# Second pass of the 64-dim head logits: 128 rows in place of 64, with hi and lo of the keys in both halves of the rows

## The chip, the cores and the metric

The kernel runs on one core of one Trainium2 chip. The metric is the time of one execution in microseconds (us), as the device measures it; the time of a kernel is the median of its runs. A profile is one execution taken by the hardware profiler. Its span is the time from the first to the last instruction of the program, and the time of a run is somewhat longer than the span.

## The reference

One layer of a streaming encoder on 512 tokens of width 1024, in float32. The same normalised input feeds three token mixers: sparse attention (branch A, 8 heads of 64), stick-breaking attention (branch B, 8 heads of 64) and cross-attention into 256 memory tokens (branch C, 4 heads of 128). Sigmoid gates merge them, and a gated feed-forward layer follows. Cut to the three places where logits of 64-dim heads are computed:

```python
def dsa_attention(aq, ak, av, iq, ik, iw, rel_bias):              # branch A
    s = einsum('bqhd,bkd->bqhk', iq_b, ik) * IDX_DIM ** -0.5      # 8 index heads of 64, one shared key
    score = einsum('bqh,bqhk->bqk', iw_b, relu(s))
    score = where(admissible[None], score, -inf)
    _, idx = top_k(score, k_sel)                                  # 128 keys of a query
    logits = einsum('bqhd,bqkhd->bhqk', aq_b, kg) * HEAD_DIM ** -0.5
    logits = logits + bias                                        # by distance, per head
    p = softmax(where(valid, logits, -inf))
    return einsum('bhqk,bqkhd->bqhd', p, vg)

def stick_breaking_attention(bq, bk, bv):                         # branch B
    z = einsum('bqhd,bkhd->bhqk', q_b, bk) * HEAD_DIM ** -0.5
    causal = kpos[None, :] < qpos[:, None]
    log_beta = log_sigmoid(z)
    log_one_minus = where(causal, log_sigmoid(-z), 0.0)
    tail = reversed_cumsum(log_one_minus) - log_one_minus
    a = where(causal, exp(log_beta + tail), 0.0)
    return einsum('bhqk,bkhd->bqhd', a, bv)

x = x + rmsnorm((g_a * ya + g_b * yb + g_c * yc) @ w_out, g_mix_post)
gu = rmsnorm(x, g_ffn_pre) @ w_ffn_in
x = x + rmsnorm((silu(gu[..., :D_FF]) * gu[..., D_FF:]) @ w_ffn_out, g_ffn_post)
```

## The kernel before

**Exact products.** Every float32 operand is split into two float32r parts, hi and lo (`split`, lines 73 to 75: a copy on ScalarE, ACT, gives hi, and a subtraction on VectorE, DVE, gives lo). A product takes three matmuls on TensorE (PE): hi with hi, hi with lo, lo with hi (`passes`, lines 81 to 87). The lines L85, L86 and L87 in the profile are these three; L206 to L208 and L731 are the same for products with tokens on the output rows. Weights come by DMA from the queue of SyncE (SP) into three buffers `wraw` (line 95) and are split into two buffers each of `wh` and `wl`.

**Logits of 64-dim heads.** Here the contraction has only 64 rows. A head's queries are therefore kept with hi in one half of the 128 rows and lo in the other (`evac_q`): the even head of a pair has hi in the lower rows, the odd head in the upper ones. One matmul of 128 rows against the hi part of the keys, which stands in both halves, gives q_hi k_hi + q_lo k_hi (line 175). A second matmul adds q_hi k_lo, on the 64 rows that hold q_hi (line 176):

```python
self.nc.tensor.matmul(out, lhsT=x[:, s], rhs=k[h % 2][:, 0:n], start=True, stop=False)
self.nc.tensor.matmul(out, lhsT=x[r, s], rhs=lo[r, 0:n], start=False, stop=True)
```

The keys come from `evac_k` for branches A and B: four tiles of two heads each. The even head's hi part goes to the lower half of one half of an `act` slot (a tile of 128 x 1024, 22 buffers), the odd head's to the upper half of the other half, and a DMA from SP copies each to the opposite half of the rows (lines 168 and 169, 64 x 512 numbers, 128 KB each). The lo parts lie in a tile `klo` of 128 x 512 (5 buffers). In the indexer the one key is shared by all heads: `index_keys` keeps hi and lo side by side in one `act` slot and copies both to the other half with one DMA (line 459), but the second pass still reads 64 rows.

**Where these pairs of matmuls stand.** There are 88. The indexer (`scores`, lines 463 to 487) has 24: 8 heads by 3 query tiles, with n = 256, 384 and 512 keys. Branches A and B have 32 each: 8 heads by 4 query tiles, with n = 128, 256, 384 and 512 keys (`heads`, lines 558 to 576).

**Order of the work.** The order on PE is that of the code (`manual_schedule`). DVE, ACT, POOL (GpSimdE) and the DMA queue of SP are put in order by a scheduler from its own costs. Independent products stand in a queue of generators, and `fill(us)` issues some of them on PE after each logits step to cover the wait for the softmax of that step. The probabilities of a head are transposed by PE (line 531), split into tiles `pt` by ACT and DVE, and multiplied with the values (line 546) one head later.

**The selection.** After the scores of a query tile, `select` finds its 128 best keys by 16 rounds of maximum and replacement on DVE (lines 502 and 503). DVE also makes all lo parts, those of the weights that PE works on meanwhile among them.

Of the kernel before, what the change touches and what calls it, by code (L numbers as in the profile page):

```python
# [17 lines left out]
P = 128  # L18
T = 512
# [16 lines left out]
# First distance of each of the 16 buckets of the relative bias.  # L36
# [3 lines left out]
def rel_onehot():  # L40
    """[32, 640] one-hot of the bucket of rel = 127 - column (a constant of the shapes)."""
    rel = 127 - np.arange(REL)
    b = np.searchsorted(np.asarray(BUCKET_START), np.abs(rel), side="right") - 1
    b = b + np.where(rel > 0, 16, 0)
    return (np.arange(32)[:, None] == b[None, :]).astype(np.float32)


class Layer:
# [32 lines left out]
    def passes(self, out, pairs, first, last):  # L81
        """out (+)= sum over pairs of (stationary hi, lo, moving hi, lo)."""
# [7 lines left out]
    def load(self, src, kc, c, tag=None):  # L90
        """src: [kc*128, c] in DRAM -> float32 tile [128, kc, c]."""
# [6 lines left out]
    def parts(self, raw, tags=None, eng=None):  # L98
        """(hi, lo) tiles of a loaded tile."""
# [10 lines left out]
    def fill(self, us):  # L110
        """issue queued work of about us microseconds."""
# [9 lines left out]
    def drain(self, *gens):  # L121
        """issue all queued work up to the last of gens (all of it without gens)."""
        while self.queue and (not gens or any(g in self.queue for g in gens)):
            self.fill(1.0)

    def mix(self, a, b, n=1):
        """b, with n steps of a after each of its steps."""
# [13 lines left out]
    def feat(self, out, w, acts, kc=NK, n=T, **kw):  # L141
        """out[c, n] = w^T acts, contraction over kc*128 features."""
# [9 lines left out]
    # Logits of 64-dim heads: hi and lo of the queries of a head fill the 128 rows of the stationary  # L152
    # operand, against the hi part of the keys in both halves; a second pass on 64 rows has the lo part
    # of the keys. The even head keeps its hi part in the lower rows, the odd one in the upper rows.
# [7 lines left out]
    def evac_k(self, ps):  # L162
        slot = self.big("act")
        e, o = slot[:, 0:T], slot[:, T:2 * T]
        lo = self.att.tile([P, T], F32R, name="klo", tag="klo", bufs=5)
        self.split(e[0:64], lo[0:64], ps[0:64])
        self.split(o[64:128], lo[64:128], ps[64:128])
        self.nc.sync.dma_start(e[64:128].bitcast(F32), e[0:64].bitcast(F32))
        self.nc.sync.dma_start(o[0:64].bitcast(F32), o[64:128].bitcast(F32))
        return e, o, lo  # L170

    def head_logits(self, out, q, k, s, h, n):
        x, lo = q[h % 2], k[2]
        r = slice(64 * (h % 2), 64 * (h % 2) + 64)
        self.nc.tensor.matmul(out, lhsT=x[:, s], rhs=k[h % 2][:, 0:n], start=True, stop=False)  # L175
        self.nc.tensor.matmul(out, lhsT=x[r, s], rhs=lo[r, 0:n], start=False, stop=True)  # L176

    def feat_tiles(self, w_src, acts, out, js, n=T, t0=0, evac=None):
        """feature-major (hi, lo) of 128-column blocks js of w_src into out[j]."""
# [14 lines left out]
    def tok_tiles(self, w_src, acts, toks, out, heads=0):  # L194
        """token-major product with [1024, 512] weights for the token tiles toks; with heads, out[t]
        is one tile of (hi, lo) per head, side by side."""
# [23 lines left out]
    def squares(self, halves, both=False):  # L220
        """[128, 2] parts of the mean square of a row, of two halves of it; on both engines if wanted."""
# [9 lines left out]
    def rstd(self, ss):  # L231
        """-2 (mean + EPS) ** -0.5 of the two parts of the mean, with one Newton step."""
# [17 lines left out]
    def normed(self, x):  # L250
        """x * rstd(x) (gain not applied)."""
# [6 lines left out]
    def run(self):  # L258
# [4 lines left out]
        with self.tc.manual_schedule(engines={mybir.EngineType.PE}):  # L263
# [6 lines left out]
            # the first 128 queries have at most 128 admissible keys: all of them are selected  # L270
# [33 lines left out]
    def setup(self):  # L304
# [11 lines left out]
        # stick-breaking: ones where key == query, sliced per query tile  # L316
# [13 lines left out]
        # relative bias by distance, times 8  # L330
# [20 lines left out]
    def transposed(self, xs, k, g, hi, lo):  # L351
        """(hi, lo) of the transposes of columns 128k.. of the token tiles xs, times the gain g."""
# [6 lines left out]
    def first(self, x, row, w_ik, w_cq):  # L359
        """h^T by halves of the tokens, with the products of the first two weight blocks after each."""  # L360
# [88 lines left out]
    def index_keys(self, cq):  # L449
        nc = self.nc  # L450
        # shared key and head weights; first block of the queries of branch C
# [3 lines left out]
        self.ik = kh, kh, kl  # L455
# [33 lines left out]
    def select(self):  # L489
        """additive masks: 0 for the 128 best admissible keys of a query, -BIG elsewhere."""  # L490
# [33 lines left out]
    def values_T(self, p, b, pT):  # L524
        """transposes of the key blocks that share bank b; p[i]: [128 queries, 128(i+1) keys]."""
# [11 lines left out]
    def values(self, pT, v, h, out):  # L537
        """out^T rows of head h = V^T P^T: V hi and lo side by side as one stationary operand."""
# [19 lines left out]
    def heads(self, prob, v, out, gap, first):  # L558
        """prob(h, i): probabilities of a query tile. The products with the values of a head come one
        head later, and queued work fills the waits."""  # L560
# [310 lines left out]
```

## Time and profile before

Three runs took 961.47, 961.82 and 962.75 us. The span of the profiled execution is 960.9 us; its own run time isn't given beside the span, and the three runs lie 0.6 to 1.9 us above that span, the median 0.9 us.

| what | value |
|---|---|
| median of the runs | 961.82 us |
| span of the profiled execution | 960.9 us |
| PE, matmuls | busy 938.7 us (98%), 4426 instructions |
| PEld, weight loads of PE | busy 760.5 us (79%), 4426 instructions |
| DVE | busy 534.3 us (56%) |
| ACT | busy 404.6 us (42%) |
| POOL | busy 107.0 us (11%) |
| DMA | 98.95 MB, 103 GB/s on the mean |
| mean granted clock of PE | 0.997 |

Consecutive matmuls overlap in the records: a matmul's recorded duration holds the time until its last result is out, while the next one has already begun. What a matmul costs in a row of them is the distance from its start to the start of the next, called its pitch here. A record such as `64*128 64x512` names the stationary operand first (64 rows by 128 columns) and then the moving one (64 rows by 512 columns). A stationary operand is loaded by an instruction of its own (PEld, LDWEIGHTS).

The stages around the change, by time from the start of the span: the indexer's pairs run from 50 to 86 us, the selection on DVE goes on until 200 us while PE works on branch C and on the projections of branch A, PE does queued products until 244 us, branch A's pairs stand between 244 and 353 us and those of branch B between 353 and 462 us.

### The profile page before, as it was taken

How to read it: one execution, taken by the hardware profiler on the slowest of the kernel's cores; microseconds unless marked ns; L12 is line 12 of the kernel's file. 1: busy time of each engine (PE TensorE's matmuls, PEld its weight loads, DVE VectorE, ACT ScalarE, POOL GpSimd, SP SyncE). 2: the span in 40 equal slices, each digit the busy share in tenths (PEclk: the TensorE clock that was granted, in tenths of full speed). 3: DMA queues.
4: the chain of work that ended last, by engine and by line, in shares of the span. 5: the costliest groups of instructions: out<-in, count | busy, mean ns of one | idle time of the engine just before them, and what ended most of it. 6: DMA issues, size and time to landing. Idle time of an engine off the chain costs nothing.

```text
span 960.9 us, 11731 instructions
## 1 busy us (share of the span) xinstructions
PE 938.7 (98%) x4426; PEld 760.5 (79%) x4426; DVE 534.3 (56%) x920; ACT 404.6 (42%) x705; POOL 107.0 (11%) x147
## 2 busy tenths in 40 slices
PE   5999999999999999999999999999999999999997
PEld 4967888888777777777788888988888888888885
DVE  7568999963587876667544477333333333322225
ACT  5354575432666555655443355322223223212122
POOL 4000000010022303334222102000000000000000
PEclk9999999999999999999999999999999999999999
DMA  7423542343343322122283536023333233332202
GB/s 226 124 63 103 154 138 78 99 110 110 109 134 109 99 67 77 44 56 66 73 267 99 176 106 201 1 76 101 88 101 97 88 102 97 110 106 92 66 23 87
DMA packets 129532, 98.95 MB, mean 103 GB/s; under 512 B 4652, under 2 KB 115292, under 8 KB 129476
## 3 DMA queue, kind: packets, MB, share of 16 engines
q1 hardware_dynamic: 128884, 97.16, 33.9%
q10 hardware_dynamic: 592, 1.05, 0.3%
q8 instruction: 34, 0.56, 0.2%
q14 instruction: 22, 0.18, 0.1%
HBM read 93.73 MB, written 2.12 MB: 100 GB/s over the span
## 4 chain that ended last, share of the span: by engine, by line
PE 88%; DVE 6%; issue 2%; DMA 1%; ACT 1%; POOL 1%; SPq 0%; DVEq 0%; POOLq 0%; ACTq 0%
PE bank L85 20%; PE bank L87 20%; PE bank L86 20%; PE bank L731 14%; PE bank L176 3%; DVE wl L75 3%; PE bank L531 2%; PE bank L546 2%; PE bank L175 2%; PE bank L206 1%; PE bank L208 1%; PE bank L207 1%; DMA act<-in_x_dram 1%; DVE score L503 1%; DMA lraw<-in_w_ffn_in_dram 1%
## 5 line engine op out<-in xcount | busy, mean ns | idle before, releaser
L75 DVE TENSOR_TENSOR wl<-wraw,wh 128x1024 fp32r<-128x1024 f32 (+1 forms) x131 | 155.1, 1185 | 177.6 <-ACT wh L74 173.2
L74 ACT CAST wh<-wraw 128x1024 fp32r<-128x1024 f32 (+1 forms) x131 | 127.2, 972 | 229.4 <-PE bank L86 163.1
L85 PE MATMUL bank<-h,wh 128*128 128x512 f32 (+1 forms) x528 | 209.6, 397 | 0.0
L87 PE MATMUL bank<-h,wl 128*128 128x512 f32 (+1 forms) x528 | 204.7, 388 | 1.0 <-DVE wl L75 0.9
L86 PE MATMUL bank<-h,wh 128*128 128x512 f32 (+1 forms) x528 | 204.4, 387 | 0.0
L87 PEld LDWEIGHTS bank<-h,wl 128*128 128x128 f32 x528 | 99.1, 188 | 22.0 <-DVE wl L75 1.7
L85 PEld LDWEIGHTS bank<-h,wh 128*128 128x128 f32 x528 | 99.3, 188 | 20.0 <-issue 1.2
L86 PEld LDWEIGHTS bank<-h,wh 128*128 128x128 f32 x528 | 99.4, 188 | 17.8
L74 ACT CAST lwh<-lraw 128x1024 fp32r<-128x1024 f32 x36 | 37.9, 1052 | 119.4 <-PE bank L86 76.2
L731 PE MATMUL bank<-lwh,act 128*128 128x512 f32 x240 | 72.6, 393 | 0.0
L731 PE MATMUL bank<-wh,act 128*128 128x512 f32 x240 | 72.5, 393 | 0.0
L75 DVE TENSOR_TENSOR lwl<-lraw,lwh 128x1024 fp32r<-128x1024 f32 x36 | 44.1, 1224 | 43.1 <-ACT lwh L74 41.3
L85 PE MATMUL bank<-h,lwh 128*128 128x512 f32 x152 | 60.1, 396 | 0.0
L86 PE MATMUL bank<-h,lwh 128*128 128x512 f32 x152 | 60.1, 396 | 0.0
L87 PE MATMUL bank<-h,lwl 128*128 128x512 f32 x152 | 60.1, 395 | 0.0
L238 POOL TENSOR_TENSOR rs<-ms,mhalf 128x1 f32<-128x1 f32 x18 | 10.4, 579 | 423.9 <-DVE ms L237 419.9
L820 DVE TENSOR_TENSOR silu<-silu,bank 128x512 f32<-128x512 f32 x22 | 15.1, 686 | 76.4 <-PE bank L87 73.6
L595 POOL TENSOR_TENSOR p<-toep,score 128x128 f32<-128x128 f32 (+3 forms) x32 | 29.8, 944 | 218.4 <-DVE score L504 112.3
L731 PEld LDWEIGHTS bank<-wh,act 128*128 128x128 f32 x240 | 45.1, 188 | 10.0
L731 PEld LDWEIGHTS bank<-lwh,act 128*128 128x128 f32 x240 | 45.1, 188 | 9.9
L74 ACT CAST act<-bank 64x512 fp32r<-64x512 f32 (+3 forms) x63 | 34.8, 552 | 38.1 <-DVE act L75 16.7
L85 PE MATMUL bank<-act,wh 128*128 128x512 f32 (+1 forms) x128 | 48.6, 380 | 0.0
(161 smaller groups left out, 1616.6 us busy)
## 6 DMA issues: line engine op xcount, KB each, us to landing
wraw<-in_w_in_dram SPq DMA_DIRECT2D x64, 512.0 KB, 3.5
wraw<-in_w_ffn_in_dram SPq DMA_DIRECT2D x22, 512.0 KB, 3.7
lraw<-in_w_ffn_in_dram SPq DMA_DIRECT2D x22, 512.0 KB, 3.7
wraw<-in_w_ffn_out_dram SPq DMA_DIRECT2D x11, 512.0 KB, 3.7
lraw<-in_w_ffn_out_dram SPq DMA_DIRECT2D x11, 512.0 KB, 3.4
wraw<-in_w_mem_kv_dram SPq DMA_DIRECT2D x8, 512.0 KB, 3.4
lraw<-in_w_out_dram SPq DMA_DIRECT2D x6, 512.0 KB, 6.3
wraw<-in_w_out_dram SPq DMA_DIRECT2D x6, 512.0 KB, 4.0
```

Of the source, the lines that this page charges most:

```text
L74: self.nc.scalar.copy(hi, src)
L75: (eng or self.nc.vector).tensor_tensor(lo, src, hi.bitcast(F32), op=OP.subtract)
L85: self.nc.tensor.matmul(out, lhsT=sh, rhs=mh, start=first and i == 0, stop=False)
L86: self.nc.tensor.matmul(out, lhsT=sh, rhs=ml, start=False, stop=False)
L87: self.nc.tensor.matmul(out, lhsT=sl, rhs=mh, start=False, stop=last and i == n - 1)
L175: self.nc.tensor.matmul(out, lhsT=x[:, s], rhs=k[h % 2][:, 0:n], start=True, stop=False)
L176: self.nc.tensor.matmul(out, lhsT=x[r, s], rhs=lo[r, 0:n], start=False, stop=True)
L531: self.nc.tensor.transpose(ps[:, c:c + P], p[i][:, j * P:(j + 1) * P], self.ident)
L546: nc.tensor.matmul(ps[:, j * P:T], lhsT=w, rhs=part[:, o:o + n], start=j == 0 and i == 0, stop=j == NT - 1 and i == 1)
L595: nc.gpsimd.tensor_tensor(s, toep[0][:, 0:n][:, ::-1], self.mask[i], op=OP.add)
L731: self.nc.tensor.matmul(ps[c], lhsT=st_[:, s], rhs=mv_[:, 0, c * 512:(c + 1) * 512], start=f and k == order[0], stop=l and k == order[-1])
L820: nc.vector.tensor_tensor(sg, sg, pss[1], op=OP.mult)
```

## The change

- `evac_k` keeps hi and lo of the keys of a head side by side in one tile of 128 x 1024: the even head in an `act` slot as before, the odd head in a tile `ko` (5 buffers) that takes the place of `klo`. Each is copied whole to the opposite half of the rows, by a DMA of 64 x 1024 numbers (256 KB). The copy of a head now waits for its lo part as well, which DVE writes.
- `head_logits` uses all 128 rows in the second matmul too, with the same stationary operand as the first. It adds q_hi k_lo + q_lo k_lo; the last term was left out before.
- In the indexer nothing more is copied: hi and lo of the key already stood in both halves.
- `ko` is twice as large as `klo`. The kernel is built with `dynamic_dma_scratch_size=1024`, where the setting was left at its default before.
- Comments and docstrings are gone, and line numbers move by up to 3.

```diff
     def evac_k(self, ps):
-        slot = self.big("act")
-        e, o = slot[:, 0:T], slot[:, T:2 * T]
-        lo = self.att.tile([P, T], F32R, name="klo", tag="klo", bufs=5)
-        self.split(e[0:64], lo[0:64], ps[0:64])
-        self.split(o[64:128], lo[64:128], ps[64:128])
-        self.nc.sync.dma_start(e[64:128].bitcast(F32), e[0:64].bitcast(F32))
-        self.nc.sync.dma_start(o[0:64].bitcast(F32), o[64:128].bitcast(F32))
-        return e, o, lo
+        e, o = self.big("act"), self.att.tile([P, 2 * T], F32R, name="ko", tag="ko", bufs=5)
+        for x, a, b in ((e, slice(0, 64), slice(64, 128)), (o, slice(64, 128), slice(0, 64))):
+            self.split(x[a, 0:T], x[a, T:2 * T], ps[a])
+            self.nc.sync.dma_start(x[b].bitcast(F32), x[a].bitcast(F32))
+        return e, o
 
     def head_logits(self, out, q, k, s, h, n):
-        x, lo = q[h % 2], k[2]
-        r = slice(64 * (h % 2), 64 * (h % 2) + 64)
-        self.nc.tensor.matmul(out, lhsT=x[:, s], rhs=k[h % 2][:, 0:n], start=True, stop=False)
-        self.nc.tensor.matmul(out, lhsT=x[r, s], rhs=lo[r, 0:n], start=False, stop=True)
+        x, y = q[h % 2][:, s], k[h % 2]
+        self.nc.tensor.matmul(out, lhsT=x, rhs=y[:, 0:n], start=True, stop=False)
+        self.nc.tensor.matmul(out, lhsT=x, rhs=y[:, T:T + n], start=False, stop=True)
...
     def index_keys(self, cq):
-        self.ik = kh, kh, kl
+        self.ik = ik, ik
...
 def kernel(**inputs):
-    nc = bacc.Bacc("TRN2", target_bir_lowering=False, num_devices=1)
+    nc = bacc.Bacc("TRN2", target_bir_lowering=False, num_devices=1, dynamic_dma_scratch_size=1024)
```

The scheduler leaves nearly all of the order as it was. Two places show what moves.

The first is the DMA queue of SP around the first two key tiles of branch A (the first lies in `act_1572`, with the change in `act_1572` and `ko_1573`; the second in `act_1673`; `wraw` are weight loads). Before:

```order
L95 DMA wraw_1681<-in_w_in_dram 128x8x128 [waits DMAHW1_49,DVE_49]
L95 DMA wraw_1717<-in_w_in_dram 128x8x128 [waits DMAHW2_49,DVE_49]
L168 DMA act_1572<-act_1572 64x512 [waits Activation_49]
L95 DMA wraw_1756<-in_w_in_dram 128x8x128 [waits DMAHW3_49,DVE_49]
L169 DMA act_1572<-act_1572 64x512 [waits Activation_49]
L95 DMA wraw_1792<-in_w_in_dram 128x8x128 [waits DMAHW4_49,DVE_49]
L168 DMA act_1673<-act_1673 64x512 [waits Activation_49]
L169 DMA act_1673<-act_1673 64x512 [waits Activation_49]
```

And with the change:

```order
L95 DMA wraw_1681<-in_w_in_dram 128x8x128 [waits DMAHW1_49,DVE_49]
L95 DMA wraw_1717<-in_w_in_dram 128x8x128 [waits DMAHW2_49,DVE_49]
L95 DMA wraw_1756<-in_w_in_dram 128x8x128 [waits DMAHW3_49,DVE_49]
L167 DMA act_1572<-act_1572 64x1024 [waits DVE_49]
L167 DMA ko_1573<-ko_1573 64x1024 [waits DVE_49]
L95 DMA wraw_1792<-in_w_in_dram 128x8x128 [waits DMAHW4_49,DVE_49]
L167 DMA act_1673<-act_1673 64x1024 [waits DVE_49]
L95 DMA wraw_1831<-in_w_in_dram 128x8x128 [waits DMAHW5_49,DVE_49]
```

The copies wait for DVE instead of ACT, and one weight load (`wraw_1756`) moves ahead of the first copy.

The second is PE at the second head of branch A, for the first query tile (n = 128; `p` are the first head's probabilities, which the four matmuls of L531, L528 with the change, transpose). Before:

```order
L87 MATMUL bank<-act,wl 128x512
L175 MATMUL bank<-act 128x128
L176 MATMUL bank<-klo,act 128x128
L531 MATMUL bank<-ident,p_2339 128x128
L531 MATMUL bank<-ident,p_2371 128x128
```

And with the change:

```order
L87 MATMUL bank<-act,wl 128x512
L172 MATMUL bank<-ko,act 128x128
L173 MATMUL bank<-ko,act 128x128
L528 MATMUL bank<-ident,p_2339 128x128
L528 MATMUL bank<-ident,p_2371 128x128
```

On PE nothing moves: 4426 matmuls in the same order, with another operand in these places.

## The prediction

> **What bounds the kernel now.** I read the page's busy times and its chain of waits first, then busy times by stage, then the timeline of PE around the pairs, because only there can one see what a single matmul costs in a row of others.
>
> ```profile
> span 960.9 us, 11731 instructions
> PE 938.7 (98%) x4426; PEld 760.5 (79%) x4426; DVE 534.3 (56%) x920; ACT 404.6 (42%) x705; POOL 107.0 (11%) x147
> PE 88%; DVE 6%; issue 2%; DMA 1%; ACT 1%; POOL 1%; SPq 0%; DVEq 0%; POOLq 0%; ACTq 0%
> ```
>
> PE is busy nearly always and makes 88% of the chain that ended last, so time taken out of PE's row of matmuls comes out of the end, as far as the engines that feed it keep up. By stage (each row: the stretch, its length, then busy us and instructions of each engine):
>
> ```profile
> core 0: us, PE busy (x) PEld busy (x) DVE busy (x) ACT busy (x) POOL busy (x), PEclk, DMA share, GB/s
> 50.00:86.00 36.00, 36.00 (x164) 24.70 (x164) 25.23 (x52) 19.41 (x40) 0.00 (x0) 1.00 0.20 59
> 86.00:200.00 114.00, 113.74 (x557) 95.13 (x556) 110.86 (x251) 62.19 (x114) 2.05 (x5) 1.00 0.40 116
> 200.00:244.00 44.00, 43.93 (x194) 36.08 (x193) 15.94 (x18) 12.93 (x17) 4.63 (x5) 1.00 0.38 108
> 244.00:353.00 109.00, 109.00 (x502) 82.62 (x502) 85.43 (x196) 67.37 (x133) 22.99 (x24) 1.00 0.38 108
> 353.00:462.00 109.00, 109.00 (x509) 82.92 (x507) 73.54 (x93) 62.81 (x127) 36.37 (x65) 1.00 0.22 62
> 279.80:294.40 14.60, 14.60 (x70) 11.17 (x69) 12.16 (x28) 10.36 (x21) 4.54 (x5) 1.00 0.61 163
> ```
>
> In branch A (244 to 353) and branch B (353 to 462) PE has no idle time and DVE has 23.6 and 35.5 us to spare. From 86 to 200 us, in the selection, DVE is nearly full too (110.9 of 114.0): there two engines bind at once, which matters for the indexer's pairs just before.
>
> **What a pair costs.** The first tile of branch A with 512 keys, on PE and on its weight loads:
>
> ```profile
> 252.57 0.39 PE L87 MATMUL bank<-act,wl 128*128 128x512 f32 x1
> 252.79 0.39 PE L175 MATMUL bank<-act 128*128 128x512 f32 x1
> 253.11 0.49 PE L176 MATMUL bank<-klo,act 64*128 64x512 f32 x1
> 253.53 0.50 PE L85 MATMUL bank<-act,wh 128*128 128x512 f32 x1
> 253.87 0.39 PE L86 MATMUL bank<-act,wh 128*128 128x512 f32 x1
> 254.10 0.40 PE L87 MATMUL bank<-act,wl 128*128 128x512 f32 x1
> ...
> 252.57 0.19 PEld L175 LDWEIGHTS bank<-act 128*128 128x128 f32 x1
> 253.11 0.18 PEld L176 LDWEIGHTS bank<-klo,act 64*128 64x128 f32 x1 [0.35 <-issue]
> 253.53 0.19 PEld L85 LDWEIGHTS bank<-act,wh 128*128 128x128 f32 x1 [0.24 <-issue]
> ```
>
> L87 to L175 and L86 to L87 show the plain pitch of a matmul of 128 rows and 512 columns: 0.22 to 0.23 us; I use 0.228. From L175 to L176 it is 0.32, from L176 to L85 0.42 and from L85 to L86 0.34. The three take 1.08 us where three plain ones take 0.684: 0.396 us too much. The loads say why. The load of L175 begins 0.22 us before its matmul, under the matmul ahead of it; those of L176 and of the L85 behind it begin together with their matmuls. So the array finishes what it holds at each change between 128 and 64 rows, and the next load is not hidden. Two passes of 128 rows, like L85 and L86, which also share a stationary operand and a bank, show none of this.
>
> The indexer shows the same sum in a full period (L175, L176 and six matmuls of 256 columns):
>
> ```profile
> 78.60 0.28 PE L86 MATMUL bank<-act,wh 128*128 128x256 f32 x1
> ...
> 79.19 0.39 PE L175 MATMUL bank<-act 128*128 128x512 f32 x1
> 79.52 0.49 PE L176 MATMUL bank<-act 64*128 64x512 f32 x1
> 79.94 0.39 PE L85 MATMUL bank<-act,wh 128*128 128x256 f32 x1
> ...
> 80.75 0.40 PE L175 MATMUL bank<-act 128*128 128x512 f32 x1
> ```
>
> From 78.60 to 79.19 five matmuls of 256 columns take 0.59, so 0.118 each. The period takes 1.56 us, and plainly it would take 2 x 0.228 + 6 x 0.118 = 1.164: 0.396 too much again. The recorded durations don't tell this (0.49 against 0.39); starts do.
>
> Narrow pairs have less to give, since what follows is slow in itself:
>
> ```profile
> 256.39 0.22 PE L175 MATMUL bank<-act 128*128 128x128 f32 x1
> 256.54 0.32 PE L176 MATMUL bank<-klo,act 64*128 64x128 f32 x1
> 256.79 0.66 PE L531 MATMUL bank<-ident,p 128*128 128x128 f32 x4
> 257.20 0.48 PE L85 MATMUL bank<-act,wh 128*128 128x512 f32 x1
> ...
> 146.13 0.60 PE L655 MATMUL bank<-ident,p 128*128 128x128 f32 x4
> 146.49 0.49 PE L85 MATMUL bank<-h,wh 128*128 128x512 f32 x1
> ```
>
> A pair of 128 columns and four transposes take 0.81 us. Four transposes with no 64-row matmul ahead take 0.36 (146.13 to 146.49). A plain pitch at 128 columns I estimate at 0.11, close to the 0.118 at 256 columns, below which the load of 128 columns seems to bind. So 0.81 - 0.36 - 0.22 = 0.23 comes free. It also shows that ahead of transposes the third step brings 0.05 (0.41 against 0.36) where it brings 0.11 ahead of L85 (0.34 against 0.228).
>
> How many there are:
>
> ```profile
> L176 PE MATMUL bank<-klo,act x64: 323/409/501, 244.2 to 461.9; 64*128 64x128 f32 x16, 64*128 64x256 f32 x16, 64*128 64x384 f32 x16, 64*128 64x512 f32 x16
> L176 PE MATMUL bank<-act x24: 379/440/500, 50.8 to 84.9; 64*128 64x256 f32 x8, 64*128 64x384 f32 x8, 64*128 64x512 f32 x8
> ```
>
> **Sum on PE.** Indexer: 24 x 0.396 = 9.5 us. Branches A and B: 48 wide pairs x 0.396 = 19.0, less 28 of them followed by transposes (7 heads x 2 branches x n = 256 and 384) x 0.06 = 1.7, plus 16 narrow pairs x 0.23 = 3.7: 21.0 us. PE gets 30.5 us shorter. Bounds of the new second pass: at best it has the plain pitch, as every other pass of 128 rows; at worst its load is exposed as that of L176 is now, 0.18 us by the row above, which takes 15.8 us from the gain (a rival below). I take the best, since it becomes the same kind of pair as L85 and L86.
>
> **What hides, what comes late.** In the indexer the logits go from PE by ACT to DVE. PE would need 36.0 - 9.5 = 26.5 us there, and DVE has 25.2 us of work in it, with waits for ACT that don't vanish. Then comes the selection, where DVE has only 3.1 us to spare and PE already waits for it here and there:
>
> ```profile
> PEld bank L207 <- DVE wl L75: 1.0, 3, 0.5
> PEld bank L546 <- DVE pt L75: 0.6, 1, 0.6
> ```
>
> So what DVE doesn't gain by 86 us, PE gives back in the selection, waiting for lo parts of weights. DVE can start earlier by at most its idle time, 10.8 us from 50 to 86. With 1 to 3 us of it staying as latency, the indexer keeps 9.5 us at best and some 4 at worst (DVE as late as now in half of the stretch); I take 8.3.
>
> In A and B the fullest head (279.8 to 294.4) has DVE at 12.16 of 14.6 us; its four pairs give 0.23 + 2 x 0.336 + 0.396 = 1.3, which leaves 13.3 us, 91% of them DVE's. The wait of L546 for `pt` shows that DVE is at times just in time. I charge 0.8 us for such waits, 0 to 4 as the range. So 20.2 us stay, and 28.5 in all: the span becomes 932.4, and with the 0.9 us by which the median of the runs shown (961.82) lies above the span, **933.3 us**.
>
> **The copies.** The prices that the trace has (SP's DMAs, the count, KB each, median us to landing; DVE's lo part of a key; and what SP's loads wait for):
>
> ```profile
> act<-act SPq DMA_DIRECT2D x16, 128.0 KB, 2.2
> act<-act SPq DMA_DIRECT2D x1, 256.0 KB, 3.0
> wraw<-in_w_in_dram SPq DMA_DIRECT2D x64, 512.0 KB, 3.5
> lraw<-in_w_out_dram SPq DMA_DIRECT2D x6, 512.0 KB, 6.3
> L75 DVE TENSOR_TENSOR klo<-bank,act x16: 676/688/695, 156.8 to 364.3; 64x512 fp32r<-64x512 f32 x16
> SPq L95 <- DVE wl L75: 389.5, 87, 34.9
> ```
>
> ACT, DVE and PE get no instruction more, and the DMAs stay 16. Each carries 256 KB, like the indexer's copy now: 0.8 us later. Each is also issued after DVE's lo part, 0.69 us or a few DVE instructions later, and the weight loads behind it on SP with it. Those loads wait 389.5 us in total for buffers that DVE frees, so they are issued as early as buffers allow; with three buffers and 24 matmuls (5.5 us) per block, an estimate of the lead is 3 x 5.5 - 3.5 for landing - 2 for the split = 11 us. A delay of 1 to 3 us lies within it: nothing. Without that cover it would cost up to 16 x 1.5 = 24 us. The copies themselves are needed when branch A starts at 244 us, 40 us after the last of A, and for B one head or more after they land: nothing.
>
> **The Trainium skill.** The page "TensorE: Matmul & The Clock Gate" speaks against this change: its section "Why this matters for your kernels" says that a single matmul with a small contraction takes as long as one with 128 rows, and "LDWEIGHTS (loading the stationary operand)" that a load of 32 rows takes as long as one of 128. The trace agrees on the load (0.18 against 0.19 us), and by that rule the time stays near 962. But "TensorEngine Tiling (Array Packing)", section "Key Properties", says that changing the tiling mode drains the array, and the starts above side with it.
>
> **Rivals.**
> *The selection takes the indexer's gain* (DVE binds from the first scores on, and PE waits in the selection for the lo parts of weights). For it: DVE at 110.9 of 114. Against: DVE idles 10.8 us before it, waiting for what PE makes. Only A and B gain: 961.8 - 20.2 = 941.6.
> *The second pass still exposes its load.* Against: L86 at plain pitch. 933.3 + 15.8 = 949.1. In the skill, "The mechanism" on the first page has a load overlap running matmuls only when row groups differ, which would make it so; the load of L175 under L87 contradicts it.
> *Rows are not the cause*, and something else at these places (the first write of a bank, the operand's place) makes the steps. Against: L85 starts a bank as well, elsewhere without steps. Then 961.8.
> *Slower: the smaller DMA scratch throttles the loads.* If they could no longer be prepared ahead, a load that lands later than the 5.5 us in which PE uses a block makes PE wait at every block. At the 6.3 us of `lraw` and with the 64 loads of `w_in` alone: 64 x 0.8 = 51 us, so 933 + 51 = 984. It decides from 5.5 + 28.5/64 = 5.95 us to landing. For it: the change makes that scratch smaller. Against: nothing in the trace shows that a load uses it.
>
> **How the numbers follow.** The forecast has a chance of 0.74, with a range of its own from 929 (no loss at all: 961.8 - 30.5 = 931.3, and 2 us for narrow pairs and waits that I priced too low) to 938 (the indexer keeps 4, and A and B lose 1.5). The selection's rival has 0.14, the exposed load 0.04, no effect 0.04, slower 0.04. For 8 in 10 the range reaches into the selection's rival: 928.5 to 942. A measurement of this kernel tells 0.2% (1.9 us) from no change. Faster: 0.74 + 0.14 + 0.04 = 0.92; same 0.04; slower 0.04.
>
> **What would show it.** L172 to L173 and on to the next matmul at 0.23 us for 512 columns, with the load of L173 starting before its matmul; the stretch of branch A at about 99 us instead of 109, that of B the same; the indexer's at 26 to 30; DVE idle time between 50 and 86 us mostly gone; the rest of the span unchanged. I am wrong if L173 keeps a pitch over 0.3, if waits for `wl` or `pt` grow by more than 3 us, or if loads of `wraw` land later than 5 us.

## The result, and the profile after

Four runs of the changed kernel took 932.92 to 935.14 us, with a median of 933.41. Four runs of the kernel before on the same chip took 961.47 to 962.75 us, with a median of 962.23. The ratio is 0.9711, with a 95% interval from 0.9697 to 0.9724: 2.9% faster. The profiled execution has a span of 933.3 us against 960.9.

From the page of the changed kernel (span, busy times, and the shares of the chain that ended last):

```profile
span 933.3 us, 11731 instructions
PE 908.5 (97%) x4426; PEld 761.9 (82%) x4426; DVE 531.7 (57%) x920; ACT 402.5 (43%) x705; POOL 109.0 (12%) x147
PE 85%; DVE 8%; issue 2%; ACT 2%; DMA 1%; POOL 1%; POOLq 0%; DVEq 0%; SPq 0%; ACTq 0%
```

The number of instructions is the same and every engine but PE has about the same work as before. PE's busy time fell by 30.2 us, from 938.7; the span fell by 27.6. DVE's share of the chain rose from 6% to 8%.

Busy times by stage of the changed kernel, in the stretches that were shown of before:

```profile
core 0: us, PE busy (x) PEld busy (x) DVE busy (x) ACT busy (x) POOL busy (x), PEclk, DMA share, GB/s
50.00:86.00 36.00, 36.00 (x226) 32.30 (x225) 32.09 (x67) 23.54 (x47) 0.00 (x0) 1.00 0.33 100
86.00:200.00 114.00, 113.66 (x535) 93.88 (x534) 108.24 (x240) 60.82 (x110) 4.88 (x9) 1.00 0.44 123
244.00:353.00 109.00, 108.21 (x552) 91.61 (x552) 91.16 (x198) 73.95 (x146) 27.49 (x30) 1.00 0.44 119
353.00:462.00 109.00, 106.42 (x538) 89.20 (x537) 73.76 (x93) 59.70 (x121) 39.84 (x63) 1.00 0.29 85
```

The stretches are the same in time and not in work: in the changed kernel the last pair of the indexer starts at 77.4 us, the pairs of branch A begin at 236.4 us and those of branch B stand between 343.7 and 435.2 us. The first 36 us now hold 226 matmuls instead of 164, and the 109 us from 244 us on 552 instead of 502. In the last stretch PE is no longer busy all the time: 2.6 us of 109 are idle, where nothing was idle before.

A pair with 512 keys and one with 128 keys on PE, in branch B of the changed kernel (start, duration, line, shapes):

```profile
422.49 0.39 PE L87 MATMUL bank<-h,wl 128*128 128x512 f32 x1
422.72 0.39 PE L172 MATMUL bank<-act 128*128 128x512 f32 x1
422.95 0.40 PE L173 MATMUL bank<-act 128*128 128x512 f32 x1
423.18 1.09 PE L543 MATMUL bank<-pt,act 128*128 128x512 f32 x5
...
427.78 0.22 PE L172 MATMUL bank<-ko,act 128*128 128x128 f32 x1
427.84 0.28 PE L173 MATMUL bank<-ko,act 128*128 128x128 f32 x1
427.95 0.62 PE L528 MATMUL bank<-ident,p 128*128 128x128 f32 x4
428.33 0.48 PE L85 MATMUL bank<-h,wh 128*128 128x512 f32 x1
```

And the weight load of the second pass in the first of them:

```profile
422.72 0.19 PEld L173 LDWEIGHTS bank<-act 128*128 128x128 f32 x1
```

Every step of the pair with 512 keys is 0.23 us, and the load of L173 begins 0.23 us before its matmul, under L172. It is so everywhere: before, all 88 loads of L176 began within 3 ns of their matmul; now each of the 88 loads of L173 begins at least 54 ns ahead of its own. The narrow pair with its four transposes takes 0.55 us (427.78 to 428.33), where it took 0.81.

The starts of the first and the last pair of each part on PE give the time of each stage (us; each number is a difference of two starts in the trace; the two columns in the middle belong to the first two experiments below):

| stage | before | indexer alone | A and B alone | changed |
|---|---|---|---|---|
| start of the span to the first pair | 50.45 | 50.78 | 52.54 | 52.09 |
| first to last pair of the indexer | 34.14 | 25.26 | 34.12 | 25.26 |
| on to the first pair of branch A | 159.45 | 159.06 | 159.48 | 159.04 |
| on to the first pair of branch B | 117.20 | 117.19 | 107.39 | 107.32 |
| on to the last pair of branch B | 100.37 | 100.38 | 91.47 | 91.48 |
| on to the end | 499.30 | 497.74 | 497.73 | 498.13 |

Before and changed differ by 8.88 us in the indexer, 0.41 in the selection and the products behind it, 9.88 in A and 8.89 in B. The first row has nothing to do with the change: three executions of the same changed program had it at 52.09, 50.73 and 50.70. What sets them apart is the granted clock. From 21.35 to 24.77 us PE ran at half clock in the first of them and at full clock in the second (the stretch, its length, busy us and instructions of PE, PEld, DVE, ACT and POOL, and then, third from the end, PEclk):

```profile
21.50:24.50 3.00, 3.00 (x15) 3.00 (x15) 2.24 (x6) 0.95 (x2) 0.00 (x0) 0.50 1.05 297
21.50:24.50 3.00, 3.00 (x28) 3.00 (x27) 2.39 (x7) 0.95 (x2) 0.00 (x0) 1.00 1.06 308
```

These 3 us hold 15 matmuls instead of 28. All 13 profiles fall in line: the five with such a stretch between 20 and 26 us have the first pair at 51.95 to 52.54 us, the other eight at 50.45 to 50.88. The last row is 1.2 us in favour of the changed kernel. All other profiles lie at or below 498.13 there, also that of the kernel before with nothing but the smaller scratch (497.37). The profile of before has its stretch at half clock there, from 586.13 to 589.55 us, so those 1.2 us are no gain. Among the 14 runs of the kernel before beside the first four experiments, the eight with a mean granted clock of 0.998 or 0.999 took 960.93 to 961.88 us and the six with 0.996 took 962.37 to 963.11, which fits one such stretch in each of the six and none in the eight.

The longest of PE's waits for other engines from 230 to 540 us, that is in branches A and B and just behind them, in the changed kernel (us in total, times, longest):

```profile
PEld bank L543 <- DVE pt L75: 2.5, 3, 1.3
PEld bank L528 <- POOL p L617: 1.6, 3, 1.0
PEld bank L528 <- DVE p L598: 1.3, 2, 0.9
```

The same view of the kernel before, from 240 to 560 us:

```profile
PEld bank L531 <- POOL p L620: 1.0, 1, 1.0
PEld bank L546 <- DVE pt L75: 0.6, 1, 0.6
```

Waits for the transposed probabilities `pt` and for the probabilities `p` have grown from 1.6 us in these two rows to 5.4.

DMA issues of the changed kernel (count, KB each, median us to landing):

```profile
wraw<-in_w_in_dram SPq DMA_DIRECT2D x64, 512.0 KB, 3.5
act<-act SPq DMA_DIRECT2D x9, 256.0 KB, 3.5
ko<-ko SPq DMA_DIRECT2D x8, 256.0 KB, 3.6
```

The copies take 1.3 to 1.4 us longer than the 2.2 us of before, and the weight loads land as they did.

### The profile page after: what moved, and what is told of

Its sections match the earlier page's. It is cut to its first block, busy times and chain, and to the rows that moved or that the text cites. A ratio compares the mean times of both kernels' runs of the same rounds, so it can differ in the third digit from the quotient of the medians.

```text
span 933.3 us, 11731 instructions
## 1 busy us (share of the span) xinstructions
PE 908.5 (97%) x4426; PEld 761.9 (82%) x4426; DVE 531.7 (57%) x920; ACT 402.5 (43%) x705; POOL 109.0 (12%) x147
## 4 chain that ended last, share of the span: by engine, by line
PE 85%; DVE 8%; issue 2%; ACT 2%; DMA 1%; POOL 1%; POOLq 0%; DVEq 0%; SPq 0%; ACTq 0%
PE bank L85 20%; PE bank L86 20%; PE bank L87 20%; PE bank L728 14%; DVE wl L75 3%; PE bank L528 2%; PE bank L543 1%; PE bank L173 1%; PE bank L172 1%; PE bank L203 1%; PE bank L205 1%; PE bank L204 1%; DVE e L615 1%; DVE score L500 1%; DMA lraw<-in_w_ffn_in_dram 1%
## 5 line engine op out<-in xcount | busy, mean ns | idle before, releaser
L74 ACT CAST lwh<-lraw 128x1024 fp32r<-128x1024 f32 x36 | 37.8, 1049 | 119.1 <-PE bank L86 76.2
L87 PE MATMUL bank<-act,wl 128*128 128x512 f32 (+1 forms) x128 | 46.5, 364 | 0.0
```

What stands on the lines that cost most here:

```text
L74: self.nc.scalar.copy(hi, src)
L87: self.nc.tensor.matmul(out, lhsT=sl, rhs=mh, start=False, stop=last and i == n - 1)
```

## The experiments

In every comparison the kernel before ran on the same chip in between; its medians were 961.37 to 962.23 us.

### Each half of the change alone

The first kernel changes only the indexer; keys of A and B are kept and multiplied as before, and the scratch is the default one (against the kernel before):

```diff
-        self.ik = kh, kh, kl
+        self.ik = ik
...
-                self.head_logits(ps[:, 0:n], iq[h // 2], self.ik, q, h, n)
+                x = iq[h // 2][h % 2][:, q]
+                nc.tensor.matmul(ps[:, 0:n], lhsT=x, rhs=self.ik[:, 0:n], start=True, stop=False)
+                nc.tensor.matmul(ps[:, 0:n], lhsT=x, rhs=self.ik[:, T:T + n], start=False, stop=True)
```

> Only the indexer's 24 second passes are on 128 rows; branches A and B are as before. Theory (each change between 128 and 64 rows drains the array, and PE is what binds): the lead over the kernel before reaches about 9 us at the end of the indexer and stays through the selection, so 953 us (951 to 955). Rival (the selection on DVE takes the indexer's gain back): over 959 us, with new waits of PE for the lo parts of weights between 86 and 200 us.

Measured: 953.19 us, ratio 0.9908 [0.9894, 0.9923].

The second kernel changes A and B and leaves the indexer on 64 rows (against the changed kernel):

```diff
-                self.head_logits(ps[:, 0:n], iq[h // 2], self.ik, q, h, n)
+                x, y, r = iq[h // 2][h % 2], self.ik[0], slice(64 * (h % 2), 64 * (h % 2) + 64)
+                nc.tensor.matmul(ps[:, 0:n], lhsT=x[:, q], rhs=y[:, 0:n], start=True, stop=False)
+                nc.tensor.matmul(ps[:, 0:n], lhsT=x[r, q], rhs=y[r, T:T + n], start=False, stop=True)
```

> Only branches A and B have the second pass on 128 rows and the wider copies; the indexer's second pass reads 64 rows as before. Theory: A and B bring 21.0 us less new waits of 1 to 3 us, so 943 us (941 to 945), and this gain and that of the indexer alone add up to that of the whole change, 28.8 us, within 1.5 us. Rival (the two gains share a cover, so that each alone is worth more or less than in the whole): their sum misses 28.8 us by over 3 us.

Measured: 944.54 us, ratio 0.982 [0.9805, 0.9835].

Each came where it was expected; their sum did not. The rival by which the selection takes the indexer's gain falls: the table above has the indexer alone at 25.26 and 159.06 us, just as in the whole change, and the selection even gives 0.4 us more. The halves are independent, as each stage of the table takes the value of the kernel whose pairs it has. The two medians save 8.66 and 17.31 us (from 961.85), 25.97 together. I had expected 28.8 within 1.5 us, so this misses by 2.8, a little less than the 3 us that the rival of a shared cover had asked for. The changed kernel's 933.41 is 28.44 below the same 961.85. Each of the three savings has an interval of 1.3 to 1.4 us to both sides, so that 2.5 us are at the edge of what can be told. Part of the gap is the clock: the four runs of the second kernel had a mean granted clock of 0.996 or 0.997, and against the six runs of the kernel before at 0.996 (median 962.66) they save 18.1 us. By stages nothing is missing: the indexer alone gains 8.88 + 0.39, A and B alone 9.81 + 8.90, 27.98 together, and the whole change 28.06 in the same four rows.

### Is it the 64 rows, or the change between 128 and 64?

The third kernel is the kernel before with both passes on 64 rows. It leaves out q_lo k_hi (against the kernel before):

```diff
-        self.nc.tensor.matmul(out, lhsT=x[:, s], rhs=k[h % 2][:, 0:n], start=True, stop=False)
+        self.nc.tensor.matmul(out, lhsT=x[r, s], rhs=k[h % 2][r, 0:n], start=True, stop=False)
```

> The kernel before with both passes of a pair on the 64 rows of q_hi: the product of q_lo and k_hi is left out. Theory (the cost sits in the change of rows, once on entering and twice on leaving): the step from the first to the second pass falls to 0.23 us at 512 columns, the step from the matmul ahead of the pair to the first pass rises to about 0.32, and the time stays at 962 us (960 to 965). Rival (a 64-row matmul is slow in itself, its load never hidden): each first pass costs some 0.2 to 0.3 us more, 88 x 0.29 = 25 us, so about 987 us. Rival (the place and not the rows: the second matmul of a bank): first to second stays at 0.32 and the time at 962.

Measured: 957.87 us, ratio 0.9961 [0.9946, 0.9975]. It is 2 us below the bound that was expected, and the step from the first pass to the second wasn't 0.23 us. PE of this kernel, first in the indexer and then in branch A with 512 keys:

```profile
53.65 0.39 PE L87 MATMUL bank<-h,wl 128*128 128x512 f32 x1
53.97 0.39 PE L175 MATMUL bank<-act 64*128 64x256 f32 x2
54.19 0.28 PE L176 MATMUL bank<-act 64*128 64x256 f32 x2
54.40 0.50 PE L85 MATMUL bank<-h,wh 128*128 128x512 f32 x1
...
248.49 0.39 PE L87 MATMUL bank<-act,wl 128*128 128x512 f32 x1
248.81 0.49 PE L175 MATMUL bank<-act 64*128 64x512 f32 x1
249.14 0.39 PE L176 MATMUL bank<-klo,act 64*128 64x512 f32 x1
249.46 0.50 PE L85 MATMUL bank<-act,wh 128*128 128x512 f32 x1
249.80 0.40 PE L86 MATMUL bank<-act,wh 128*128 128x512 f32 x1
```

The four steps from 248.49 to 249.80 are 0.32, 0.33, 0.32 and 0.34 us (medians over this kernel's pairs: 0.318, 0.337, 0.323, 0.34). Above the plain 0.228 that is 0.09, 0.11, 0.095 and 0.11: 0.41 for two passes on 64 rows, as much as for one such pass in the kernel before. So the price belongs to the change, and it is the same in both directions: about 0.09 us on the step into the new number of rows, and 0.11 on the step after it. The single 64-row matmul of before had both on one step: 0.228 + 0.11 + 0.09 = 0.43 us, and 0.42 was seen. On 64 rows itself nothing is slower. The rival by which the rows aren't the cause falls with the indexer alone (first kernel): there the second pass differs from that of before in nothing but the rows, with the same bank and the same tile of keys, and 8.88 us went. A and B gained nothing here: the two rows of the table that hold them are 117.66 and 100.78 us, against 117.20 and 100.37. Between the first pair of the indexer and the first of A the kernel saved 5.5 us. My expectation had left out two things there. Nine of the 24 pairs stand right behind another one and, on 64 rows, share its visit, so that there are 15 visits instead of 24: some 9 x 0.40 = 3.6 us. The rest fits matmuls that run two at a time: heads next to each other use opposite halves of the rows, and in the rows with x2 above their matmuls start 7 ns apart.

That changes between modes of tiling drain the array is what the Trainium skill says ("TensorEngine Tiling (Array Packing)", "Key Properties"). The trace agrees that each such change costs time, and adds the price: 0.20 us here. That it is a drain is the page's word; the rows show loads that begin only with their matmuls.

### The same price, twice as often

Two kernels cut every pair into two halves of the columns: the one on 128 and 64 rows in turn, as before (so four changes for a pair instead of two), the other on 128 rows only, as a control for what the added instructions cost. Against the kernel before and against the changed kernel:

```diff
-        self.nc.tensor.matmul(out, lhsT=x[:, s], rhs=k[h % 2][:, 0:n], start=True, stop=False)
-        self.nc.tensor.matmul(out, lhsT=x[r, s], rhs=lo[r, 0:n], start=False, stop=True)
+        for c in (slice(0, n // 2), slice(n // 2, n)):
+            self.nc.tensor.matmul(out[:, c], lhsT=x[:, s], rhs=k[h % 2][:, c], start=True, stop=False)
+            self.nc.tensor.matmul(out[:, c], lhsT=x[r, s], rhs=lo[r, c], start=False, stop=True)
```

```diff
-        self.nc.tensor.matmul(out, lhsT=x, rhs=y[:, 0:n], start=True, stop=False)
-        self.nc.tensor.matmul(out, lhsT=x, rhs=y[:, T:T + n], start=False, stop=True)
+        for c in (0, n // 2):
+            o = out[:, c:c + n // 2]
+            self.nc.tensor.matmul(o, lhsT=x, rhs=y[:, c:c + n // 2], start=True, stop=False)
+            self.nc.tensor.matmul(o, lhsT=x, rhs=y[:, T + c:T + c + n // 2], start=False, stop=True)
```

> The kernel before with each pair done in two halves of the columns: first and second pass on the first n/2 keys, then both on the rest, so that PE goes to 64 rows and back twice per pair. Compared with e7, which has the same halves on 128 rows alone. Theory (a fixed price for each visit to 64 rows): the difference is about twice that of one visit each, 176 visits x 0.25 to 0.40 = 44 to 70 us, so 990 to 1012 us. Rival (64 rows stream slower, by the column): the difference stays at 28 us, 972 us.

> The changed kernel with each pair done in two halves of the columns, all on 128 rows. Narrow matmuls have a floor of about 0.11 us, so halves of 64 to 192 columns cost more than the whole: some 11 us in all, 944 us (939 to 950). This is the control for e6; both theories expect the same of it.

Measured: 998.82 us with the visits doubled, ratio 1.0403 [1.0347, 1.0459], and 955.83 us for the control, ratio 0.9938 [0.9923, 0.9953]. The control was expected at 944 and missed by 12 us. The difference of the two is 43.0 us: 1 us under the theory's lower bound of 44, 15 above the rival's 28. The four runs with the visits doubled spread from 996.40 to 1009.40 us, so that this difference is known to some 6 us.

PE of the kernel with doubled visits, at a pair with 512 keys:

```profile
265.46 0.28 PE L176 MATMUL bank<-act 128*128 128x256 f32 x1
265.67 0.38 PE L177 MATMUL bank<-klo,act 64*128 64x256 f32 x1
265.98 0.38 PE L176 MATMUL bank<-act 128*128 128x256 f32 x1
266.29 0.38 PE L177 MATMUL bank<-klo,act 64*128 64x256 f32 x1
266.61 0.51 PE L85 MATMUL bank<-act,wh 128*128 128x512 f32 x1
266.95 0.40 PE L86 MATMUL bank<-act,wh 128*128 128x512 f32 x1
```

And of the control, also with 512 keys:

```profile
267.56 0.28 PE L174 MATMUL bank<-ko,act 128*128 128x256 f32 x1
267.68 0.28 PE L175 MATMUL bank<-ko,act 128*128 128x256 f32 x1
267.80 0.28 PE L174 MATMUL bank<-ko,act 128*128 128x256 f32 x1
267.92 0.28 PE L175 MATMUL bank<-ko,act 128*128 128x256 f32 x1
```

From 265.46 to 266.95 the first takes 1.49 us. Plainly it would be 4 x 0.118 + 0.228 = 0.70 us. The 0.79 too much are four changes of 0.20 us. The control has the plain step of 0.12 throughout. So the price per change is the same at 256 columns as at 512, and doesn't shrink when changes stand close together.

The control was slow mostly for another reason. Its waits of PE for other engines are longer than in the changed kernel:

```profile
PEld bank L545 <- DVE pt L75: 3.5, 6, 1.2
PEld bank L87 <- DVE wl L75: 3.4, 4, 1.2
PEld bank L530 <- DVE p L600: 2.9, 3, 1.4
PEld bank L174 <- DVE act L79: 2.8, 1, 2.8
```

These four make 12.6 us, where the same four waits of the changed kernel make 5.5 (2.5, 1.7, 1.3 and none). All rows of this view together make 36.2 us, against 26.0 in the changed kernel. So waits account for some 10 of the 12 us of the miss. I had priced the added matmuls on PE, but not that the waits would grow with them.

The difference of 43 us is therefore blurred by waits that only the control has. PE's starts don't have this fault. The steps that begin with a matmul of the pairs, each from its start to the next start on PE, add up to 53.5 us in the kernel before and 28.5 in the changed one, 25.0 apart (the 0.11 us on the step after each visit isn't in this sum). With the pairs halved they add up to 89.0 and 37.8 us, 51.1 apart. So twice the visits cost twice as much, within the theory's range of 44 to 70; and the added matmuls of the control cost 9.3 us on PE, near the 11 that were expected.

### Copies and scratch

The copies of the keys made twice (against the changed kernel):

```diff
-            self.nc.sync.dma_start(x[b].bitcast(F32), x[a].bitcast(F32))
+            for _ in range(2):
+                self.nc.sync.dma_start(x[b].bitcast(F32), x[a].bitcast(F32))
```

> The changed kernel with each of the 16 copies of the keys issued twice. Theory (the copies lie under the lead of the weight loads and are needed late): 933.4 us within 1.5 us. Rival (the wider copies hold back the loads behind them on SP): the second set costs what the first did, at least 2 us more, with waits of ACT for weight loads between 150 and 365 us.

Measured: 934.19 us, ratio 0.9707 [0.9691, 0.9724], and the changed kernel in the same series, run for comparison:

> The changed kernel once more, for a second profile. Theory (the 1.6 us by which the first indexer pair came late in the profile of the change, and the 1.5 us won near 600 us, belong to the execution and not to the change): 933.4 us within 1 us, and the first pair at 50 to 53 us. Rival (the change delays the start): the first pair at 52.1 us again within 0.2 us, as in no profile of the kernel before.

It took 934.07 us, ratio 0.9709 [0.9695, 0.9724].

DMA issues of the kernel with doubled copies:

```profile
act<-act SPq DMA_DIRECT2D x17, 256.0 KB, 3.0
ko<-ko SPq DMA_DIRECT2D x16, 256.0 KB, 3.6
```

Sixteen copies more, and 0.12 us; between 150 and 365 us the trace lists no wait of ACT for a weight load. So the copies are hidden with room to spare.

The kernel before with the smaller scratch and nothing else:

```diff
-    nc = bacc.Bacc("TRN2", target_bir_lowering=False, num_devices=1)
+    nc = bacc.Bacc("TRN2", target_bir_lowering=False, num_devices=1, dynamic_dma_scratch_size=1024)
```

> The kernel before with the smaller DMA scratch and nothing else. Theory (no load uses it): 962 us within 1 us, weight loads landing in 3.5 us. Rival (it slows or speeds the loads): landing moves by over 0.5 us, and the time by over 2 us.

Measured: 962.76 us as the median of nine runs from 960.94 to 963.51 (a tenth took 3223.56 us, for a reason that isn't known, and is left out), ratio 1.0003 [0.9993, 1.0013]. Weight loads land in 3.6 us. The scratch does nothing here, and the rival falls.

### Can the new waits be covered?

The changed kernel reaches each head's softmax sooner, and the waits for `pt` and `p` grew. Two kernels issue more queued work behind each logits step (`GA` and `GB` for A and B) and after the first head of A (`FA`), to see whether that takes the waits away. The third of the series is the changed kernel itself, for comparison.

```diff
-GA, GB = 2.05, 1.85
-FS, FM, GC, FC, FA, FB, FW, FT, FR = 0.7, 50, 1.8, 2.0, 1.00, 2.20, 17.00, 14, 0.65
+GA, GB = 2.05, 1.95
+FS, FM, GC, FC, FA, FB, FW, FT, FR = 0.7, 50, 1.8, 2.0, 2.0, 2.2, 17.00, 14, 0.65
```

```diff
-GA, GB = 2.05, 1.85
-FS, FM, GC, FC, FA, FB, FW, FT, FR = 0.7, 50, 1.8, 2.0, 1.00, 2.20, 17.00, 14, 0.65
+GA, GB = 2.3, 2.0
+FS, FM, GC, FC, FA, FB, FW, FT, FR = 0.7, 50, 1.8, 2.0, 2.0, 2.2, 17.00, 14, 0.65
```

> The changed kernel with more queued work per step: GB 1.95 instead of 1.85 in branch B, and FA 2.0 instead of 1.0 after the first head of branch A. Theory (the waits of PE for p and pt in A and B, about 4.9 us in the profile of the change, are there because each step's cover has become 0.3 to 0.4 us shorter): the wait of 0.87 us at the first head of A goes, those within B get shorter, and the time falls by 1 to 2 us to about 932. Rival (the queue is only emptied earlier, and the wait moves to the end of B): within 0.5 us of the changed kernel.

> As e9, with GA 2.3 instead of 2.05 in branch A and GB 2.0 in branch B. Theory: as in e9, and the two short waits in A go too, 931 to 932 us. Rival (queue emptied earlier, later waits longer): 934 us or more.

> The changed kernel on the same chip as e9 and e10, for comparison: 933.5 us within 1 us by both.

Measured: 937.01 us for the first, ratio 0.9744 [0.9731, 0.9757]; 942.65 for the second, ratio 0.98 [0.9785, 0.9815]; 933.55 for the change beside them, ratio 0.9715 [0.9701, 0.9729]. My theory falls: more cover made it slower, by 3.5 and 9.1 us. The rival of the first (within 0.5 us of the change) falls too; that of the second (934 us or more, with longer waits later) came true.

The waits didn't go away, they grew. All waits of PE's loads that the trace lists from 230 to 520 us add up to 5.8 us in the change, 9.4 in the first and 12.5 in the second kernel. The place is seen best in the second, on PE at the end of branch A:

```profile
341.24 0.51 PE L528 MATMUL bank<-ident,p 128*128 128x128 f32 x3
344.95 0.98 PE L528 MATMUL bank<-ident,p 128*128 128x128 f32 x7 [3.19 <-DVE p L598]
...
350.11 0.63 PE L87 MATMUL bank<-h,wl 128*128 128x512 f32 x1
350.53 0.63 PE L85 MATMUL bank<-h,wh 128*128 128x512 f32 x1
```

In the change, six queued matmuls stand between the transposes of the last head and its values at this place (L528 at 339.54, L543 at 341.14 in its profile of this series). Here the queue is empty: the work was issued earlier, and the last head has none left, so PE waits 3.19 us for DVE to finish `p`. Behind this wait comes a second loss, told by the granted clock (the stretch, its length, the busy times, and then, third from the end, PEclk):

```profile
345.50:346.00 0.50, 0.43 (x4) 0.20 (x2) 0.01 (x1) 0.50 (x2) 0.00 (x0) 1.00 0.00 0
348.00:352.00 4.00, 4.00 (x14) 3.42 (x13) 2.36 (x4) 3.20 (x6) 0.00 (x0) 0.50 0.46 100
353.50:354.00 0.50, 0.50 (x5) 0.42 (x4) 0.00 (x0) 0.00 (x0) 0.00 (x0) 1.00 0.00 0
```

In half-microsecond stretches the clock is at half from about 346.4 to 353.2 us, and a matmul of 512 columns took 0.42 to 0.43 us per step (350.11 to 350.53) instead of 0.228. Half of 6.8 us is 3.4. With 12.5 - 5.8 = 6.7 us of waits that makes 10.1 us, and the spans differ by 9.7 (941.3 and 931.6). For the first kernel the waits give 3.6, and the spans differ by 3.2. So where the time went is shown; that the last wait comes from cover used up too early is read from the rows of this one place, and no run tried it by itself. The Trainium skill gives the rule for the clock ("TensorE: Matmul & The Clock Gate", "Why this matters for your kernels"): no idle gaps of PE over about 3 us. The traces agree only in part, and shorter gaps are no safety. After 3.19 us the clock fell, and after the 1.63 us that were the longest wait in the first kernel's branches it didn't. But half clock for 3.4 us also followed a wait of 1.66 us in the profile of the changed kernel (until 21.05 us; in eight of the 13 profiles the same wait had no such consequence) and one of 1.38 us in the profile of before (until 585.34). A wait of 2.57 us in the control with halves on 128 rows (until 71.88) had none. And in the kernel with doubled visits PE was busy without a break from 60 to 77 us and still fell to half clock from 77.31 to 80.72. What sets the clock, and whether the wait of 3.19 us caused its fall, stays open.

No version tried here beats the change.

## Why the prediction was right

The time was forecast at 933.3 us and measured at 933.41, and the mechanism was the one forecast: the second pass on 64 rows cost 0.4 us per wide pair in changes of rows, and PE's time came out of the end. That the two numbers agree to 0.1 us is luck, as some terms were off and cancelled.

**The price of a pair** was right: 0.396 us too much per wide pair, and after the change 0.23 us at every step. The *reading* of its three steps was incomplete. I took the load that isn't hidden in the second pass for the drain. The kernel with both passes on 64 rows shows two equal changes per pair, each 0.09 us into it and 0.11 us after it. For this change the sum is the same, so the forecast didn't suffer; for the experiment with 64 rows it did.

**Narrow pairs** were priced a little low: 0.23 us forecast, 0.26 measured (0.81 to 0.55). The estimate of 0.11 us per matmul at 128 columns was too high for the first pass, which takes 0.06 us (427.78 to 427.84), and right for the second.

**The indexer** kept more than forecast: 8.88 + 0.41 = 9.3 us instead of 8.3, of 9.5 us on PE. DVE's idle time from 50 to 86 us went from 10.8 to 3.9 us (from about 77 us on this stretch is the selection already), so DVE did start earlier, and the selection lost nothing. The charge of 1.2 us for latency was not needed.

**Branches A and B** kept less: 9.88 us in A and 8.89 in B up to its last pair, 18.8 instead of 20.2, and 0.3 us less again at the last head's wait (the 500th matmul behind the start of the last pair comes 113.74 us after it, before 113.41). The mis-sized term is the 0.8 us that I charged for new waits. With the narrow pairs at 0.26 us, PE got 19.0 - 1.7 + 16 x 0.26 = 21.5 us shorter, so nearly 3 us were lost, within the range of 0 to 4 that I gave. The rows say where: waits for `pt` and `p` in these stages grew by 3 to 4 us. I had looked at the fullest head of A, and none of them is there. They are spread: 0.9 us at the first head of A (L528 for `p`), 1.2 at two heads in the middle of B (L543 for `pt`), 0.7 more than before at the last head of B (1.3 instead of 0.6), and smaller ones. At the last of these DVE splits a block of weights (2.29 us) and makes a scan (0.94 us) ahead of `pt`.

**The copies and the scratch** cost nothing, as said; the runs with doubled copies and with the scratch alone show it. The copies land 1.3 to 1.4 us later than before, where 0.8 was forecast, without consequence.

**The sum.** The terms of the pairs come to 9.3 + 18.4 = 27.7 us instead of 28.5. The profile of the changed kernel also began 1.64 us later and that of before lost some 1.5 us behind the branches, each with a stretch of 3.4 us at half clock, and the two nearly cancel in the spans. The medians differ by 28.8 us, which is 27.7 within their interval of 1.3 us. The 0.9 us that I added to the span is not the distance between a run and its own span: where both are recorded that is 1.8 us (935.14 and 933.3), one more term that was off.

**The rivals.** The selection doesn't take the indexer's gain (953.19 us for the indexer alone). The second pass doesn't expose its load (0.23 us per step, and the load of L173 runs under L172 on the same rows, against the rule of the Trainium skill that the prediction named). The rows are the cause, by way of the change between them (8.88 us in the indexer alone, where nothing else was changed). The scratch doesn't throttle the loads (ratio 1.0003).

## What to carry to other kernels

A matmul on 64 rows between matmuls of 128 rows isn't free, though its recorded duration looks ordinary: read the distance between starts for it and for the *two* matmuls around it. If the free rows of the array can be filled with something useful or harmless (here q_lo k_lo), the change of mode goes away, here at no cost that the runs show; if not, put all the small matmuls one behind the other, since the price is per change and not per matmul. And when PE's part of a stage shrinks, look at the last iteration, where no queued work is left to cover the waits that then come due.

## What the runs showed of the hardware that I had not expected

- The price of a change is symmetric and the same at 512 columns as at halves of 256: 0.09 us into it and 0.11 us on the next matmul, 0.20 in all. At 128 columns ahead of transposes, two changes cost 0.26 us together and not 0.40.
- Two matmuls on opposite halves of the rows (even and odd head in the indexer of the third kernel) are recorded with starts 7 ns apart, in the rows with x2 above, and ran at the same time. In those rows the two changes take back what that gives: from 53.97 to 54.40 four such matmuls of 256 columns take 0.43 us, where four in a row on 128 rows take 4 x 0.118 = 0.47. Away from a change it is a full factor of two. From 63.32 to 63.49 us two matmuls of 384 columns together take 0.17 us, as much as one on 128 rows (0.176).
- A wait of PE of 3.19 us was followed, some 1.5 us after PE had begun again (344.95), by 6.8 us at half clock. Stretches of 3.4 us at half clock came behind waits of 1.66 and 1.38 us in other executions, and once with no wait of PE at all.
- The start of the program up to its first pair varied by 2.1 us among profiles (50.45 to 52.54), by whether 3.4 us of it ran at half clock. Differences of 2 us between spans say nothing before the stages and their granted clocks are compared.
